# Last position tile's accumulators in three banks, and the last norm's means on VectorE

## The chip, the core and the metric

The kernel runs on one core of one Trainium2 chip. The metric is the device time of one execution in microseconds (us). TensorE (PE) multiplies into eight PSUM banks of 512 float32 columns; ScalarE (ACT), VectorE (DVE) and GpSimd (POOL) do the rest; SyncE (SP) issues every DMA.

## The reference, cut to what matters

One decoder block over 256 positions of 1024 features: two attention branches merged by gates, then a gated feed-forward part with a short causal convolution, then a last norm. The change touches only the last lines:

```python
h = rmsnorm(x, ffn_norm[l])
u = causal_dwconv(h @ w_up[l], conv_w[l], conv_b[l])
x = x + (jax.nn.silu(u[..., :D_FF]) * u[..., D_FF:]) @ w_down[l]
...
return rmsnorm(x, final_norm)      # x * rsqrt(mean(x * x) + 1e-6) * final_norm
```

## The kernel before, in words

Every float32 product on TensorE is three float32r passes: each operand is split into a rounded part (hi) and the rest (lo), and hi*hi, hi*lo and lo*hi are summed in PSUM (mm3, line 333). Weights stream through SBUF once in units of 1 MB (line 345), in three raw, three hi and three lo buffers; ScalarE copies hi, VectorE subtracts lo.

The feed-forward part has 2816 hidden features, in 11 groups g of 256. For each group two up units (line 783) compute 128 + 128 features by 256 positions: 8 K tiles, 2 halves, 3 passes, so 48 products of 256 columns each, with the weights as the stationary operand. VectorE and ScalarE then convolve and gate them and leave ph and pl. A down unit (line 821) contracts the group's two K tiles into the residual: positions lie on partitions, so the stationary operand is ph or pl, 128 positions of it, and the weights move past, 512 columns at a time. Four accumulators stay open over all 11 groups: position tile tt (0 or 1) by half n (0 or 1) of the 1024 output columns, those of tile 0 in banks of the ring sc, those of tile 1 in the two banks of the ring av. The ring sc has three banks, the ring mm three, av two. A down unit goes over K outermost; the last one goes over accumulators outermost (line 835), so that the banks close one after the other.

finish(tt), line 839, ends the kernel for a position tile: per half an add of the accumulator to x2 on VectorE and a square with a sum on ScalarE; then on GpSimd two tensor_scalar that form mean + EPS and one power to -0.5; the product of all 1024 columns with the norm's weights fn on VectorE; then y times r, 640 columns on VectorE and 384 on ScalarE, each stored by a DMA of its own from SP's queue. y is the tile B8 (B in the rows), x2 and fn lie in the tile gate, sums and means in smalls, squares go to tb.

Nothing is emitted in the order in which it is recorded. A planner (Program, lines 143 to 256) gives each instruction a price (line 277), and each engine in turn takes the oldest of its recorded instructions whose operands are there by those prices: 0.8 us after the last product for what reads TensorE's results, 0.15 us after another engine's instruction. SP alone keeps the order of recording. Instructions run in the emitted order on their engine and wait there for their operands. Everything is emitted from line 242, so all rows have that line and are told apart by tiles. These are the prices that matter, for n columns:

```python
return passes * max(0.107, 0.0025 + args[0].shape[1] / 2400)   # TensorE
return 0.1 + n * 0.833e-3 + 0.09 * more                        # ScalarE
return 0.63 if kw.get("op") == ALU.pow else 0.15 + n * 2.25e-3 # GpSimd
return 0.1 + n * 0.52e-3                                       # VectorE tensor_scalar
return (0.13 if method == "scalar_tensor_tensor" else 0.07) + n * 1.04e-3
```

Of the kernel before, what the change touches and what calls it, by code (L numbers as in the profile page):

```python
"""Hybrid MLA + MoBA block with a ConvFFN on one core.

Every float32 product on the tensor engine is three float32r passes: both operands are split
into a part rounded to float32r and the exact rest (hi*hi + hi*lo + lo*hi, summed in PSUM).
Weights stream through SBUF once, in the order of their use, and are split on the way.
Activations stay on chip, features on partitions where they are contracted next.

MoBA: SEQ equals MOBA_BLOCK, so there is one block, none lies in the past of any query, every
selected score is masked and what is left is causal attention within the block.
"""  # L10
# [17 lines left out]
D = 1024  # L28
S = 256
# [9 lines left out]
# columns of the small parameters  # L39
# [4 lines left out]
def unit_plan():  # L44
    """The weights in the order of their use: (kind, index)."""
    plan = [("lat", 0), ("lat", 1), ("lat", 2)]
    plan += [("v", n) for n in range(4)]
    plan += [("q", 0), ("gate", 0), ("k", 0), ("gate", 1), ("q", 1), ("gate", 2), ("k", 1)]
    plan += [("q", 2), ("gate", 3), ("k", 2), ("gate", 4), ("q", 3), ("gate", 5), ("k", 3)]
    plan += [("gate", 6), ("mqk", 0), ("gate", 7), ("mv", 0), ("mqk", 1), ("ob", 0), ("mqk", 2)]  # L50
    plan += [("mqk", 3), ("ob", 1)]
    plan += [("ob", 2), ("ob", 3)]
    plan += [("oa", i) for i in range(4)]
    plan += [("out", n) for n in range(4)]
    for g in range(FT // 2):
        plan += [("up", 2 * g), ("up", 2 * g + 1)]
        if g:
            plan += [("down", g - 1)]
    plan += [("down", FT // 2 - 1)]
    return plan  # L60
# [3 lines left out]
SIZE = {"mqk": 3 * 384 + 2 * 256}  # the others have UNIT columns  # L64


def pack_weights(w_in, w_uq, w_ukv, w_o_mla, w_o_moba, w_out, w_up, w_down):
    """Layout alone: each unit as [128 rows of K, column group, K tile, columns of the group]."""
# [9 lines left out]
    # rotated halves lie 64 partitions apart: [x1, x1, x2, x2]  # L78
# [40 lines left out]
def rope_tables():  # L119
    """cos and the signed sin by [row, position]; rows r and r + 64 are a rotated pair."""  # L120
# [11 lines left out]
def constants():  # L132
    """Tables that depend on shapes alone: rope, the identity, the causal mask of a block, the
    rows of the first and of the second head in a pair's rotated tile."""
    p = np.arange(128)
    mask = np.where(p[None, :] <= p[:, None], 0.0, -1e30).astype(np.float32)
    sel = np.stack([(p // 32) % 2 == 0, (p // 32) % 2 == 1], axis=1).astype(np.float32)
    return np.ascontiguousarray(
        np.concatenate([*rope_tables(), np.eye(128, dtype=np.float32), mask, sel], axis=1)
    )  # L140


class Program:
    """Instructions, recorded in the order of the computation and emitted in the order of a
    simple model of the engines: each engine takes the oldest of its instructions whose operands
    are there. What reads or writes the same part of a tile keeps its order, and so do functions
    of the scalar engine with tables of their own."""

    LATENCY = {"tensor": 0.8}  # others 0.15
    DMA_LATENCY = 1.6  # L150

    def __init__(self, nc):
        self.nc = nc
        self.ops = []  # [engine, cost, calls, dependencies]
        self.users = {}  # tile -> [(op, region, writes)]
# [8 lines left out]
    def together(self):  # L164
        """Instructions of one engine that stay together."""
# [42 lines left out]
    def emit(self):  # L208
# [16 lines left out]
        for _ in range(n):  # L225
            best = None
            for e, js in open_ops.items():
                if not js:
                    continue
                if e == "sync":  # a queue  # L230
                    js = [j for j in js if j == min(loads)]
                    if not js:
                        continue
# [36 lines left out]
def region(ap):  # L270
    """Partitions and elements of a tile that an access covers."""
# [5 lines left out]
def price(engine, method, args, kw):  # L277
    """Microseconds, about."""
# [20 lines left out]
def hybrid_block(ctx: ExitStack, tc: tile.TileContext, xT, x, par, con, fnorm, wpack, out):  # L299
# [9 lines left out]
    class Ring:  # L309
        """Tiles that take turns."""  # L310
# [32 lines left out]
    units = iter(range(len(PLAN)))  # L343

    def weights(kind, i, *cuts):
        """The next unit's two parts, split in pieces that end at the cuts."""
# [56 lines left out]
    def rsqrt(dst, src, n, width):  # L403
        """(src / n + EPS) ** -0.5"""
# [13 lines left out]
    def to_rows(o, col2):  # L418
        """[128 positions, 2] -> the same S values on every partition, in PSUM o [128, S]."""
# [5 lines left out]
    def feature_tile(o, m, w, ah, al, ks, first, last):  # L425
        """128 columns' products into half m of bank o: [features, positions]."""
# [4 lines left out]
    def proj_pair(kind, i, ah, al, *cuts):  # L431
        """Two feature tiles of 128 columns into one bank."""
# [9 lines left out]
    def proj_tokens(kind, i0, o, ah, al, *between):  # L442
        """[positions, 512 columns] in two banks, K outermost."""
# [20 lines left out]
    def rope(o, n, cos, sin):  # L464
        """o [128, n * S]; rows r and r + 64 rotate together."""
# [14 lines left out]
    # the gates' tile holds the latents before, the residual and the last weights after  # L480
# [56 lines left out]
    def lat_sums(j, tt):  # L537
        """Sums of squares over the features of a latent, by position."""
# [27 lines left out]
    # the rotated shared key, for the first and the second head of a pair: rows of the other are 0  # L566
# [11 lines left out]
    def attention(i, q, k, more, scale, vh, vl, yh, yl):  # L578
        """q, k, more: (hi, lo) of [features, 2, S]; of more queries [features, S] that the heads'
        keys, zero in the other's rows, select from."""  # L580
        heads = range(2)
        # [position of a query, its tile's keys of both heads]: 128 of the first tile, all of the second
# [28 lines left out]
        for hh in heads:  # L611
# [3 lines left out]
            # blocks (query, key): (0, 0), (1, 0), (1, 1)  # L615
# [116 lines left out]
    def to_features(ks):  # L732
        """x2's columns, features on partitions, by the norm's weights, split."""
# [24 lines left out]
    # half 0: K outermost, as the merged tiles arrive  # L758
# [5 lines left out]
    # half 1: one tile of positions after the other  # L764
# [18 lines left out]
    def up_unit(i, ph, pl):  # L783
        """u's two tiles, convolved; the gated product, split."""
# [30 lines left out]

    acc = {}
    fn = gate[:, 0:4].rearrange("p a b -> p (a b)")
    y = b8
    ss3, r3 = small(4), small(2)

    def down(g, ph, pl):
        wv = groups(weights("down", g), 2, D)
        if not acc:
            for tt in range(2):
                for n in range(2):
                    acc[tt, n] = (sc_bank, av_bank)[tt]()

        def product(tt, n, k):
            kk = 2 * g + k
            t, c = slice(128 * tt, 128 * tt + 128), slice(512 * n, 512 * n + 512)  # L830
            mm3(acc[tt, n], ph[:, k, t], pl[:, k, t], wv[0][:, 0, k, c], wv[1][:, 0, k, c],
                kk == 0, kk == FT - 1)

        order = [(tt, n, k) for k in range(2) for tt in range(2) for n in range(2)]
        for tt, n, k in order if g < FT // 2 - 1 else sorted(order):
            with P.together():
                product(tt, n, k)

    def finish(tt):
        """The last residual and norm."""  # L840
        for n in range(2):
            c = slice(512 * n, 512 * n + 512)
            dve.tensor_add(x2[:, tt, c], acc[tt, n], x2[:, tt, c])
            squares(x2[:, tt, c], ss3[:, 2 * tt + n : 2 * tt + n + 1])
        v, r = small(2), r3[:, tt : tt + 1]
        pool.tensor_scalar(v[:, 0:1], ss3[:, 2 * tt : 2 * tt + 1], 1.0 / D, EPS, op0=ALU.mult,
                           op1=ALU.add)
        pool.tensor_scalar(v[:, 1:2], ss3[:, 2 * tt + 1 : 2 * tt + 2], 1.0 / D, v[:, 0:1],
                           op0=ALU.mult, op1=ALU.add)
        pool.tensor_tensor(r, v[:, 1:2], mhalf[:, 0:1], op=ALU.pow)  # L850
        dve.tensor_mul(y[:, tt], x2[:, tt], fn)
        a, b = slice(0, 640), slice(640, D)
        dve.tensor_scalar(y[:, tt, a], y[:, tt, a], r, None, op0=ALU.mult)
        sp.dma_start(out[:, tt, a], y[:, tt, a])
        act.activation(y[:, tt, b], y[:, tt, b], AF.Copy, scale=r)
        sp.dma_start(out[:, tt, b], y[:, tt, b])
# [48 lines left out]
```

## Time and profile before

| | us |
|---|---|
| median of three runs | 450.98 |
| lowest and highest of them | 450.87, 451.32 |
| span of the profiled execution | 450.0 |
| TensorE busy in it | 439.0 (98%) |
| VectorE, ScalarE, GpSimd busy | 356.7, 274.8, 10.8 |
| TensorE's share of the chain that ended last | 96% |

The span runs from the first to the last instruction of the profiled execution; the time of a run holds a little more. TensorE's busy time is made of records whose ends are modelled and overlap. The chain that ended last goes back from the last instruction, at each step to what released it.

### The profile page before, as it was taken

The page shows a single profiled execution, that of the slowest core. Times are in us where ns is not written, and L with a number is a line of the kernel's source. Part 1 is how long each engine was busy: PE and PEld are TensorE (multiplying, and loading weights), DVE is VectorE, ACT ScalarE, POOL GpSimd, SP SyncE. Part 2 cuts the span into 40 slices and gives each one's busy share as a digit, 9 for nine tenths or more (in the row PEclk, how much of TensorE's full clock was granted, in tenths as well). Part 3 has the DMA queues.
Part 4 walks back from the last instruction along what each step waited for, and adds up shares of the span by engine and source line. Part 5 has one row for each costly group of instructions (what it writes and reads, how often), then busy time and mean ns, then how long its engine had stood idle before and what let it go on. Part 6 is the DMA issues. An engine that isn't in the chain of part 4 may idle for free.

```text
span 450.0 us, 8134 instructions
## 1 busy us (share of the span) xinstructions
PE 439.0 (98%) x3302; PEld 415.4 (92%) x3302; DVE 356.7 (79%) x548; ACT 274.8 (61%) x475; POOL 10.8 (2%) x26
## 2 busy tenths in 40 slices
PE   7999999999999999999999999999999999999993
PEld 4988999999999999999998899999999999999982
DVE  3767998888987988793788568997887797797764
ACT  5786446546554766877765558765565565565523
POOL 0010300000000000000000010000000000000002
PEclk9999999999999999999999999999999999999998
DMA  6994745455254434240288454375555555556002
GB/s 197 399 402 162 263 155 184 178 183 181 90 185 165 137 124 182 93 174 17 105 340 302 188 188 137 144 288 197 190 201 203 192 205 198 197 192 233 2 1 93
DMA packets 13861, 81.77 MB, mean 182 GB/s; under 512 B 1664, under 2 KB 2560, under 8 KB 5120
## 3 DMA queue, kind: packets, MB, share of 16 engines
q1 hardware_dynamic: 13824, 81.25, 49.9%
q8 instruction: 26, 0.43, 0.4%
q14 instruction: 11, 0.09, 0.1%
HBM read 80.20 MB, written 1.05 MB: 181 GB/s over the span
## 4 chain that ended last, share of the span: by engine, by line
PE 96%; DMA 1%; SPq 1%; ACT 1%; POOL 1%; issue 0%; DVE 0%; POOLq 0%; ACTq 0%
PE mm L242 69%; PE av L242 14%; PE sc L242 12%; DMA raw<-in_wpack 1%; SPq L242 1%; POOL smalls L242 1%; ACT tb L242 0%; DVE gate L242 0%; ACT B L242 0%; POOLq L900 0%; ACT whi L242 0%; POOLq L242 0%; ACTq L242 0%
## 5 line engine op out<-in xcount | busy, mean ns | idle before, releaser
L242 ACT CAST whi<-raw 128x1024 fp32r<-128x1024 f32 (+3 forms) x158 | 152.3, 978 | 86.0 <-PE mm L242 70.3
L242 DVE TENSOR_TENSOR wlo<-raw,whi 128x1024 fp32r<-128x1024 f32 (+3 forms) x158 | 175.8, 1129 | 34.6 <-ACT whi L242 33.9
L242 PE MATMUL mm<-XH,whi 128*128 128x256 f32 x656 | 184.4, 281 | 1.8 <-ACT whi L242 1.8
L242 PE MATMUL mm<-XH,wlo 128*128 128x256 f32 x656 | 182.7, 278 | 0.0
L242 PE MATMUL mm<-XL,whi 128*128 128x256 f32 x656 | 182.5, 278 | 0.0
L242 PEld LDWEIGHTS mm<-XH,whi 128*128 128x128 f32 x656 | 124.3, 189 | 2.7 <-ACT whi L242 2.3
L242 PEld LDWEIGHTS mm<-XL,whi 128*128 128x128 f32 x656 | 124.2, 189 | 0.5
L242 PEld LDWEIGHTS mm<-XH,wlo 128*128 128x128 f32 x656 | 124.4, 190 | 0.2 <-DVE wlo L242 0.2
L242 DVE SCALAR_TENSOR_TENSOR tb<-ta,prm,tb 128x255 f32<-128x255 f32 x88 | 40.4, 480 | 2.2 <-ACT tb L242 0.7
L242 ACT ACTIVATE tb<-ta,prm 128x256 f32<-128x256 f32 x44 | 24.3, 595 | 3.8 <-DVE ta L242 3.8
L242 ACT ACTIVATE e<-sc,smalls 128x128 f32<-128x128 f32 (+1 forms) x32 | 13.3, 419 | 12.6 <-DVE smalls L242 11.7
L242 DVE TENSOR_TENSOR ta<-ta,tb 128x256 f32<-128x256 f32 (+1 forms) x35 | 16.9, 484 | 2.2 <-ACT ta L242 0.7
L242 ACT CAST qh<-ta 128x256 fp32r<-128x256 f32 (+1 forms) x26 | 11.4, 437 | 11.8 <-DVE ta L242 11.7
L242 DVE TENSOR_TENSOR ta<-mm,rbc 128x512 f32<-128x512 f32 x22 | 15.2, 689 | 4.2 <-PE mm L242 4.2
L242 PE MATMUL mm<-YBH,whi 128*128 128x256 f32 x64 | 18.1, 283 | 0.0
L242 PE MATMUL mm<-YBH,wlo 128*128 128x256 f32 x64 | 17.7, 277 | 0.0
L242 PE MATMUL mm<-VH,whi 128*128 128x256 f32 x64 | 17.7, 277 | 0.0
L242 PE MATMUL mm<-YBL,whi 128*128 128x256 f32 x64 | 17.7, 277 | 0.0
L242 PE MATMUL mm<-VL,whi 128*128 128x256 f32 x64 | 17.7, 276 | 0.0
L242 PE MATMUL mm<-VH,wlo 128*128 128x256 f32 x64 | 17.7, 276 | 0.0
L242 PE MATMUL sc<-whi,ql 128*128 128x512 f32 x44 | 17.3, 394 | 0.0
L242 PE MATMUL av<-whi,ql 128*128 128x512 f32 x44 | 17.3, 394 | 0.0
(167 smaller groups left out, 735.1 us busy)
## 6 DMA issues: line engine op xcount, KB each, us to landing
raw<-in_wpack SPq DMA_DIRECT2D x66, 1024.0 KB, 4.8
raw<-in_wpack SPq DMA_DIRECT2D x4, 832.0 KB, 4.2
raw<-in_wpack SPq DMA_DIRECT2D x7, 256.0 KB, 6.6
raw<-in_wpack SPq DMA_DIRECT2D x2, 512.0 KB, 5.2
B<-in_x SPq DMA_DIRECT2D x1, 1024.0 KB, 10.0
gate<-in_x SPq DMA_DIRECT2D x1, 1024.0 KB, 4.8
raw<-in_xT SPq DMA_DIRECT2D x3, 256.0 KB, 6.1
cst<-in_con SPq DMA_DIRECT2D x1, 641.0 KB, 11.1
```

The source lines that it names most:

```text
L242: getattr(getattr(self.nc, e), method)(*args, **kw)
```

## The change

The accumulators become five parts: tile 0 keeps two banks of 512 columns (both sc), tile 1 gets 512 and 256 columns in the two av banks and 256 columns in the third sc bank. The products follow these parts, in the same order as before. In finish, the squares are scaled by D ** -0.5 each (a square of the input times 1/32), so that their sums are means; VectorE adds EPS to the first mean, adds the means up, and multiplies each part with the norm's weights when it is there; GpSimd keeps only the power. The final scaling is in three cuts, 0 to 384 and 384 to 640 on VectorE, 640 to 1024 on ScalarE, with the same two stores. Comments were also taken out of the file, which moves its lines.

```diff
+    parts = [(0, slice(0, 512)), (0, slice(512, D)),
+             (1, slice(0, 512)), (1, slice(512, 768)), (1, slice(768, D))]
     acc = {}
...
-    ss3, r3 = small(4), small(2)
+    r3 = small(2)
...
         if not acc:
-            for tt in range(2):
-                for n in range(2):
-                    acc[tt, n] = (sc_bank, av_bank)[tt]()
-
-        def product(tt, n, k):
+            for j, b in enumerate((sc_bank, sc_bank, av_bank, av_bank, sc_bank)):
+                acc[j] = b()
+
+        def product(j, k):
             kk = 2 * g + k
-            t, c = slice(128 * tt, 128 * tt + 128), slice(512 * n, 512 * n + 512)
-            mm3(acc[tt, n], ph[:, k, t], pl[:, k, t], wv[0][:, 0, k, c], wv[1][:, 0, k, c],
-                kk == 0, kk == FT - 1)
-
-        order = [(tt, n, k) for k in range(2) for tt in range(2) for n in range(2)]
-        for tt, n, k in order if g < FT // 2 - 1 else sorted(order):
+            tt, c = parts[j]
+            t = slice(128 * tt, 128 * tt + 128)
+            mm3(acc[j][:, : c.stop - c.start], ph[:, k, t], pl[:, k, t], wv[0][:, 0, k, c],
+                wv[1][:, 0, k, c], kk == 0, kk == FT - 1)
+
+        order = [(j, k) for k in range(2) for j in range(len(parts))]
+        for j, k in order if g < FT // 2 - 1 else sorted(order):
             with P.together():
-                product(tt, n, k)
+                product(j, k)
 
     def finish(tt):
-        """The last residual and norm."""
-        for n in range(2):
-            c = slice(512 * n, 512 * n + 512)
-            dve.tensor_add(x2[:, tt, c], acc[tt, n], x2[:, tt, c])
-            squares(x2[:, tt, c], ss3[:, 2 * tt + n : 2 * tt + n + 1])
-        v, r = small(2), r3[:, tt : tt + 1]
-        pool.tensor_scalar(v[:, 0:1], ss3[:, 2 * tt : 2 * tt + 1], 1.0 / D, EPS, op0=ALU.mult,
-                           op1=ALU.add)
-        pool.tensor_scalar(v[:, 1:2], ss3[:, 2 * tt + 1 : 2 * tt + 2], 1.0 / D, v[:, 0:1],
-                           op0=ALU.mult, op1=ALU.add)
-        pool.tensor_tensor(r, v[:, 1:2], mhalf[:, 0:1], op=ALU.pow)
-        dve.tensor_mul(y[:, tt], x2[:, tt], fn)
-        a, b = slice(0, 640), slice(640, D)
-        dve.tensor_scalar(y[:, tt, a], y[:, tt, a], r, None, op0=ALU.mult)
-        sp.dma_start(out[:, tt, a], y[:, tt, a])
-        act.activation(y[:, tt, b], y[:, tt, b], AF.Copy, scale=r)
-        sp.dma_start(out[:, tt, b], y[:, tt, b])
+
+        mine = [j for j in range(len(parts)) if parts[j][0] == tt]
+        means = small(len(mine))
+        for i, j in enumerate(mine):
+            c = parts[j][1]
+            n = c.stop - c.start
+            dve.tensor_add(x2[:, tt, c], acc[j][:, :n], x2[:, tt, c])
+            act.activation(tbs().rearrange("p a s -> p (a s)")[:, :n], x2[:, tt, c], AF.Square,
+                           scale=D ** -0.5, accum_out=means[:, i : i + 1])
+
+            if i < len(mine) - 1:
+                if i:
+                    dve.tensor_add(means[:, i : i + 1], means[:, i : i + 1], means[:, i - 1 : i])
+                else:
+                    dve.tensor_scalar(means[:, 0:1], means[:, 0:1], EPS, None, op0=ALU.add)
+                dve.tensor_mul(y[:, tt, c], x2[:, tt, c], fn[:, c])
+        v, r = small(1), r3[:, tt : tt + 1]
+        dve.tensor_add(v, means[:, -1:], means[:, -2:-1])
+        c = parts[mine[-1]][1]
+        pool.tensor_tensor(r, v, mhalf[:, 0:1], op=ALU.pow)
+        dve.tensor_mul(y[:, tt, c], x2[:, tt, c], fn[:, c])
+        cuts = (0, 384, 640, D)
+        for q, (a, b) in enumerate(zip(cuts, cuts[1:])):
+            if q < 2:
+                dve.tensor_scalar(y[:, tt, a:b], y[:, tt, a:b], r, None, op0=ALU.mult)
+            else:
+                act.activation(y[:, tt, a:b], y[:, tt, a:b], AF.Copy, scale=r)
+        sp.dma_start(out[:, tt, :640], y[:, tt, :640])
+        sp.dma_start(out[:, tt, 640:], y[:, tt, 640:])
```

## Rows read from the trace of the kernel before

**Rows 1.** The page's first line.

```profile
span 450.0 us, 8134 instructions
```

**Rows 2.** Busy time by stretch: nine feed-forward rounds; columns are named in its first line.

```profile
core 0: us, PE busy (x) PEld busy (x) DVE busy (x) ACT busy (x) POOL busy (x), PEclk, DMA share, GB/s
289.04:436.64 147.60, 147.60 (x1082) 138.74 (x1081) 121.88 (x183) 84.81 (x125) 0.00 (x0) 1.00 0.51 182
```

**Rows 3.** The chain that ended last, in order of time: start us, us, what.

```profile
420.24 10.91 PE mm L242 x96
431.15 1.37 PE sc L242 x6
...
443.49 1.16 POOL smalls L242
...
445.68 0.62 ACT B L242
```

**Rows 4.** Timeline of PE: start us, us, instruction; the last of tile 1's two accumulators.

```profile
440.37 0.39 PE L242 MATMUL av<-whi,ql 128*128 128x512 f32 x1
...
441.74 0.40 PE L242 MATMUL av<-whi,ql 128*128 128x512 f32 x1
```

**Rows 5.** Timeline of DVE in the tail.

```profile
438.06 0.69 DVE L242 TENSOR_TENSOR gate<-sc,gate 128x512 f32<-128x512 f32 x1 [2.16 <-PE sc L242]
439.43 0.69 DVE L242 TENSOR_TENSOR gate<-sc,gate 128x512 f32<-128x512 f32 x1 [0.68 <-PE sc L242]
440.15 1.23 DVE L242 TENSOR_TENSOR B<-gate 128x1024 f32<-128x1024 f32 x1
441.30 0.68 DVE L242 TENSOR_TENSOR gate<-av,gate 128x512 f32<-128x512 f32 x1
442.18 0.55 DVE L242 TENSOR_SCALAR B<-B,smalls 128x640 f32<-128x640 f32 x1 [0.20 <-POOL smalls L242]
442.65 0.69 DVE L242 TENSOR_TENSOR gate<-av,gate 128x512 f32<-128x512 f32 x1
443.37 1.23 DVE L242 TENSOR_TENSOR B<-gate 128x1024 f32<-128x1024 f32 x1
445.68 0.55 DVE L242 TENSOR_SCALAR B<-B,smalls 128x640 f32<-128x640 f32 x1 [1.09 <-POOL smalls L242]
```

**Rows 6.** Timeline of POOL in the tail.

```profile
441.60 0.55 POOL L242 TENSOR_TENSOR smalls<-smalls,mhalf 128x1 f32<-128x1 f32 x1
443.49 1.52 POOL L242 TENSOR_SCALAR smalls<-smalls 128x1 f32<-128x1 f32 x2 [1.35 <-ACT tb L242]
445.09 0.55 POOL L242 TENSOR_TENSOR smalls<-smalls,mhalf 128x1 f32<-128x1 f32 x1
```

**Rows 7.** The page's costliest groups: busy us, mean ns of one, idle before.

```profile
L242 PEld LDWEIGHTS mm<-XH,whi 128*128 128x128 f32 x656 | 124.3, 189 | 2.7 <-ACT whi L242 2.3
```

**Rows 8.** Groups by line and shape of DVE and ACT: busy us, mean ns, idle before.

```profile
L242 DVE TENSOR_TENSOR ta<-ta,tb 128x256 f32<-128x256 f32 x27 | 11.4, 423 | 2.0 <-ACT ta L242 0.7
...
L242 DVE TENSOR_SCALAR smalls<-smalls 128x2 f32<-128x2 f32 x16 | 2.7, 170 | 0.5
...
L242 DVE TENSOR_SCALAR diag<-cst,smalls 128x128 f32<-128x128 f32 x8 | 2.0, 284 | 4.1 <-POOL smalls L242 4.0
...
L242 ACT ACTIVATE ta<-tb 128x256 f32<-128x256 f32 x22 | 9.1, 413 | 2.9 <-DVE tb L242 2.8
```

**Rows 9.** Timeline of ACT: the square of tile 0's second half.

```profile
440.21 0.63 ACT L242 ACTIVATE tb<-gate 128x512 f32<-128x512 f32 x1 [0.71 <-DVE gate L242]
440.75 0.18 ACT L242 ACTIVATION_READ_ACCUMULATOR tb<-gate 128x1 f32 x1
```

**Rows 10.** Timeline: earlier powers on POOL, the DVE subtraction beside the first.

```profile
47.19 1.22 DVE L242 TENSOR_TENSOR wlo<-raw,whi 128x1024 fp32r<-128x1024 f32 x1
47.21 1.74 POOL L242 TENSOR_TENSOR smalls<-smalls,mhalf 128x2 f32<-128x2 f32 x1
...
263.52 0.69 POOL L242 TENSOR_TENSOR smalls<-smalls,mhalf 128x2 f32<-128x2 f32 x1
```

**Rows 11.** Timeline of SP's queue: the last two stores.

```profile
446.26 0.81 SPq L242 DMA_DIRECT2D out<-B  x2
```

## The prediction

> **What bounds the kernel now.** I read the page first: 450.0 us of span [rows 1]. The time to predict, 450.98 us, is the median of three runs; about 1.0 us of it lies outside the span. I make the sum on the span and keep that 1.0 us. 0.2% of the time, 0.9 us, is about what a measurement of this kernel can tell from no change. Next, the stretches: in nine rounds of the feed-forward part TensorE is busy 147.60 of 147.60 us at granted clock 1.00, its 2.4 GHz level [rows 2]. There, only what TensorE itself takes counts. Then the chain that ended last [rows 3]: TensorE all the way, then a tail that TensorE doesn't set. Its last product starts at 441.74 and is done at 442.14 [rows 4]; the last ScalarE and VectorE scalings end at 446.30 and 446.23 [rows 3, 5]. So the change can act in two places: TensorE's rounds, and the 4.1 us from its end to the last store, with some 3.7 us of store and closing behind them.
>
> The tail is seen in VectorE's rows [rows 5]. It ran add 0, add 1, weights' product of tile 0 (1.23), add 2, the scaling of tile 0 (442.18), add 3 (442.65), product of tile 1, scaling of tile 1. Add 3 could have started at 442.14 and began 0.5 late, as the scaling stood ahead of it. Behind it come two squares, two means on GpSimd and the power. Of the means the first took 1.16 us [rows 3] and the power 0.55, from 445.09 to 445.64 [rows 6].
>
> **Part 1, the shorter products.** In each of 11 down units, the 2 K tiles by 3 passes by 1 half of 512 columns make 66 products; they become 132 of 256. TensorE's price: 96 products of 256 columns took 10.91 us, 113.6 ns each; six of 512 took 1.37 us, 228.3 ns [rows 3]. Two short ones are 227.3, so 66 pairs come to 0.07 us less. The weight load of a short product lasts 189 ns [rows 7], more than 113.6, but the 96 of a round are each preceded by one and don't show it. What the trace lacks is short products whose stationary side is the activations; as bounds I take -0.1 us and, should a load show through, the third rival below. I take -0.07, as the nearest row is the same shape in the same round.
>
> The Trainium skill (TensorE: Matmul & The Clock Gate, Back-to-back issue gap) gives an isolated warm matmul N/2.4 ns plus about 2.5 ns, so each of the 66 extra products would cost that; the forecast would be 0.24 us higher, about 451.0. The trace doesn't agree: 113.6 and 228.3 ns lie 7 and 15 ns above N/2.4, an excess in proportion and not per product.
>
> The fifth accumulator takes the third of the score banks, last read at the start of the feed-forward part; nothing waits for it.
>
> **Part 2, the order.** The planner emits each engine's oldest ready instruction by its own prices (lines 208 to 256, 277 to 295), so the order can be worked out from the code. Count from its start of the last down unit: the banks close at 1.295, 2.590, 3.885, 4.540, 5.195, and an add may start 0.8 later. VectorE then takes add 0 (2.095), product 0 (2.697), add 1 (3.390), EPS, product 1 (4.093), add 2 (4.695), the sum for tile 0 (5.298), product 2 (5.369), add 3 (5.971, 256 columns). At 6.308 it is free; tile 0's power is planned out at 6.299, so tile 0's two scalings are ready and are the oldest. They go first, then tile 1's first mean, product 3, and only then add 4, ready since 5.995. The same working on the kernel before gives exactly the order of [rows 5]. ScalarE: squares 0, 1, 2, tile 0's scaling, squares 3, 4, tile 1's scaling.
>
> So add 4, whose bank closes at 442.14, still stands behind tile 0's scalings, as add 3 did, and now also behind a product. That is where I look for the gain to go.
>
> **Part 3, the tail with measured durations.** VectorE's spacing, from [rows 5]: an instruction follows an independent one 0.08 us before its end (scaling 442.18, 0.55 long; add 442.65) and one that it reads 0.03 after it. Durations: 512 columns 0.69 [rows 5], 256 columns 0.42; a scalar scaling 0.28 for 128 columns [rows 8] and 0.55 for 640 [rows 5], so by the line between them 0.42 for 384 and 0.35 for 256: the split costs two starts, 0.69 - 0.55 = 0.14 us in all. A one-column operation is not shown on VectorE; two columns take 0.17 [rows 8]; bounds 0.07 (it is overlapped) and 0.17; I take 0.17 where it is waited for, 0.07 where not. A square with its sum took 0.72 for 512 (440.21 to 440.93) [rows 9]; 256 columns save 0.63 - 0.41 [rows 8, 9], so 0.51.
>
> With TensorE's end as it was: add 1 439.43; EPS 440.04; product 1 440.15; add 2, whose bank closes at 440.76 [rows 4], 440.80; the sum for tile 0 441.41 to 441.58; product 2 441.49 to 442.18; add 3 442.10 to 442.52. GpSimd's power for tile 0 could start at 441.60, as before [rows 6], but product 2, of two SBUF operands, is running. What that does is seen earlier: a power beside a weights' subtraction (two SBUF operands, 1.22 us) took 1.74 us against 0.69 with VectorE idle [rows 10]; it ends about 0.6 after the subtraction does. The 1.16 us mean under the product at 443.37 is the same [rows 3, 5]. So the power ends 0.55 after 442.1, near 442.64, not at 442.15, and VectorE waits for it. Unknown between 0 and 0.5 us; I take it in full, as product 2 starts 0.1 earlier than the power.
>
> Scaling of 384 at 442.67, of 256 at 443.01, first mean 443.28, product 3 443.35, add 4 443.69 to 444.11 (then product 4 hidden behind the square); square 4 444.17 to 444.68; sum 444.73 to 444.90; power 444.92 to 445.47, VectorE idle beside it; scalings 445.50 and 445.84 to 446.19. Before, the last VectorE scaling ended at 446.23: -0.04. ScalarE's ends near 446.1; the two stores go out one behind the other on SP's queue as before (446.26, 0.81 for both) [rows 11], so their first one sets them.
>
> What goes: four GpSimd means, two of which were on the path (443.49 to 445.02). What takes their place: add 4, 1.55 us after its bank closed. Freed and re-spent are nearly equal. Sum: 450.98 - 0.07 - 0.04 = 450.9; I say 450.8, as the one-column operations are charged at their upper bound, 0.1 each at two places, of which I take half.
>
> **The rivals.** (a) The power isn't held up by product 2. For it: the sum for tile 0 may come out before product 2 has really begun; against it: [rows 10]. VectorE then goes from add 3 straight to the scaling at 442.44, 0.23 sooner, and all behind it: 450.6. (b) The adds follow their banks: if add 3 and add 4 are emitted ahead of tile 0's scalings, add 4 runs 442.17 to 442.59, square to 443.16, sum, power to 443.95, scalings to 444.67: 1.5 us less, 449.3. Against it: by the planner's prices the scalings are ready 0.009 us before VectorE is free, and even if they weren't, one short mean would go in between and the scalings next; only a different planned state of VectorE at the start would do it. (c) Slower: the 132 short products show their weight loads, as the loads stand at 189 ns against 113.6. At full exposure 132 x 0.075 = 9.9 us, 460.8; it decides from 7 ns for each (0.9 us), 451.9. Against it: the 96-product runs. (d) Longer queue: GpSimd gets in only after add 3 too, VectorE idle until then: 0.4 us more, 451.2.
>
> **How the numbers follow.** Forecast 0.55 (450.8, its own range 450.5 to 451.1); (a) 0.15; (b) 0.12; (c) 0.08; (d) 0.10. (a), (d) and the forecast lie within 0.2%: 0.80, less 0.01 for a low end of (a): 0.79. Faster: (b) and that 0.01, 0.13. Slower: (c), 0.08. The range reaches past (a), 450.6, by the 0.45 us between the runs shown, to 450.2, and past (d) to 451.4, leaving (b) and (c) out.
>
> **What would show it.** Right: in the chain of the changed kernel TensorE's down stretches within 0.1 us of before; on VectorE two scalings between add 3 and add 4; tile 0's power about 1.0 us long, tile 1's 0.55; tile 1's last add more than 1 us after TensorE's end; the first of the last stores issued near 446.1. Wrong: a wait of TensorE inside the rounds (its longer planned products can shift the planner's order there; one misplaced weights' subtraction is worth up to 1.2 us, hidden now since TensorE waits for nothing), a clock below 1.00, or add 4 right behind add 3.

## The result, and the profile after

The changed kernel takes 455.8 us (median of six runs, 454.95 to 457.44) against 451.15 before in the same runs: a ratio of 1.0098, 95% interval 1.0078 to 1.0119. It is slower by 1%, outside the range of the prediction. The profiled execution's span is 454.1 us against 450.0. Two executions among those of the experiments (742.71 and 743.44 us, granted clock 0.56) are in none of the ratios.

The chain that ended last shows where it goes. One round of the feed-forward part after (start us, us, what):

```profile
288.88 11.31 PE mm L242 x96
300.19 1.40 PE sc L242 x6
301.59 1.05 PE av L242 x6
302.65 1.74 PE sc L242 x9
304.39 1.03 PE av L242 x6
305.41 0.34 PE sc L242 x3
305.75 11.31 PE mm L242 x96
```

A round takes 16.87 us (288.88 to 305.75) instead of 16.40 [rows 2, 3]; nine of them make 4.2 us. Most of it is in the first line: 96 products of two up units, which the change doesn't touch, take 11.31 us instead of 10.91 [rows 3], 117.8 ns each instead of 113.6. The down part has grown too, from 5.49 (16.40 - 10.91) to 5.56 (16.87 - 11.31). Its last products, ahead of the next stretch, are at the old spacing again (the last line ahead of 305.75: three of 256 columns in 0.34 us), so each round takes up the wider spacing anew. Busy time by stretch, two rounds after and the first of these rounds before:

```profile
core 0: us, PE busy (x) PEld busy (x) DVE busy (x) ACT busy (x) POOL busy (x), PEclk, DMA share, GB/s
288.88:305.75 16.87, 16.87 (x129) 16.09 (x128) 16.62 (x25) 10.20 (x16) 0.00 (x0) 1.00 0.76 283
305.75:322.63 16.88, 16.88 (x129) 16.10 (x128) 13.53 (x21) 9.64 (x14) 0.00 (x0) 1.00 0.55 194
```

```profile
289.04:305.44 16.40, 16.40 (x123) 15.42 (x122) 16.15 (x25) 10.18 (x16) 0.00 (x0) 1.00 0.75 285
```

TensorE is busy throughout, at granted clock 1.00 as before [rows 2], and no wait of TensorE stands in the trace in these rounds: the products simply follow each other more widely. The load around them doesn't explain it: a round with 0.76 of the DMA time and one with 0.55 take the same, and before, 0.75 went with 16.40. Below, "narrow" and "wide" are the two spacings: 113.6 and 117.8 ns for 256 columns, 228.3 and 233.3 (1.40 us for six) for 512. Said of a product itself, "short" is 256 and "wide" 512 columns.

The tail, by contrast, is as forecast. TensorE's last product, VectorE and GpSimd after:

```profile
445.94 0.28 PE L242 MATMUL sc<-whi,ql 128*128 128x256 f32 x1
```

```profile
445.50 0.15 DVE L242 TENSOR_TENSOR smalls<-smalls 128x1 f32<-128x1 f32 x1
445.62 0.69 DVE L242 TENSOR_TENSOR B<-gate 128x512 f32<-128x512 f32 x1
446.23 0.42 DVE L242 TENSOR_TENSOR gate<-av,gate 128x256 f32<-128x256 f32 x1
446.75 0.68 DVE L242 TENSOR_SCALAR B<-B,smalls 128x384 f32<-128x384 f32 x2
447.35 0.15 DVE L242 TENSOR_SCALAR smalls<-smalls 128x1 f32<-128x1 f32 x1
447.42 0.42 DVE L242 TENSOR_TENSOR B<-gate 128x256 f32<-128x256 f32 x1
447.75 0.42 DVE L242 TENSOR_TENSOR gate<-sc,gate 128x256 f32<-128x256 f32 x1
...
449.63 0.68 DVE L242 TENSOR_SCALAR B<-B,smalls 128x384 f32<-128x384 f32 x2 [0.67 <-POOL smalls L242]
```

```profile
445.73 0.99 POOL L242 TENSOR_TENSOR smalls<-smalls,mhalf 128x1 f32<-128x1 f32 x1 [181.68 <-DVE smalls L242]
449.04 0.55 POOL L242 TENSOR_TENSOR smalls<-smalls,mhalf 128x1 f32<-128x1 f32 x1 [2.32 <-DVE smalls L242]
```

Tile 0's scalings (446.75) stand between add 3 (446.23) and add 4 (447.75), whose bank closed at 446.22. Tile 0's power took 0.99 us under the product at 445.62, tile 1's 0.55 with VectorE idle. From TensorE's end to the end of the last VectorE scaling: 446.22 to 450.31, 4.09 us; before, 442.14 to 446.23 [rows 4, 5], 4.09.

### The profile page after: what moved, and what is told of

The parts are those of the page before. It is cut to its first block, busy times and chain, and to the rows that moved or that the text cites. A ratio compares the mean times of both kernels' runs of the same rounds, so it can differ in the third digit from the quotient of the medians.

```text
span 454.1 us, 8273 instructions
## 1 busy us (share of the span) xinstructions
PE 443.2 (98%) x3368; PEld 422.0 (93%) x3368; DVE 358.3 (79%) x559; ACT 274.8 (61%) x477; POOL 9.3 (2%) x22
## 4 chain that ended last, share of the span: by engine, by line
PE 95%; DMA 1%; issue 1%; DVE 1%; SPq 1%; POOL 0%; POOLq 0%; ACT 0%; DVEq 0%
PE mm L242 69%; PE sc L242 13%; PE av L242 13%; DMA raw<-in_wpack 1%; SPq L242 1%; DVE B L242 0%; DVE gate L242 0%; POOL smalls L242 0%; POOLq L915 0%; ACT whi L242 0%; DVEq L915 0%; DVE smalls L242 0%
## 5 line engine op out<-in xcount | busy, mean ns | idle before, releaser
L242 PE MATMUL sc<-whi,ql 128*128 128x512 f32 (+1 forms) x66 | 23.5, 356 | 0.0
L242 PE MATMUL sc<-wlo,qh 128*128 128x512 f32 (+1 forms) x66 | 23.5, 355 | 0.0
L242 PE MATMUL sc<-whi,qh 128*128 128x512 f32 (+1 forms) x66 | 23.5, 355 | 0.0
```

The costliest lines, as they stand in the source:

```text
L242: getattr(getattr(self.nc, e), method)(*args, **kw)
```

## The experiments

In what follows a stretch is the 96 products of two up units, a seam the step from a down unit to the next up unit. Nine seams lead to a stretch. "Seam products" are what stands between two stretches.

**The tail alone** (e1_tail_only): four accumulators as before, the new finish.

```diff
-             (1, slice(0, 512)), (1, slice(512, 768)), (1, slice(768, D))]
+             (1, slice(0, 512)), (1, slice(512, D))]
...
-            for j, b in enumerate((sc_bank, sc_bank, av_bank, av_bank, sc_bank)):
+            for j, b in enumerate((sc_bank, sc_bank, av_bank, av_bank)):
```

> The new last residual and norm alone, on four accumulators of 512 columns as before. The changed kernel's feed-forward rounds take 16.87 us against 16.40 before, and every product in most of them stands 4 to 5 ns further from the next, those of the unchanged up units too. Theory A (the short products of the down units bring it on): rounds of 16.40 again, 113.6 ns per product in the stretches of 96, and the time within 0.3 us of before, 450.7 to 451.3. Rival R (the new tail's code or the planner's order brings it on): rounds near 16.87, 454 to 456.

Measured 450.89 against 451.64, ratio 0.9983 (0.9964 to 1.0002); all stretches narrow. Theory R falls. Its tail is even shorter than that of before: TensorE's end at 441.28, last scaling's end at 444.67, 3.39 us against 4.09. The last add starts 0.03 us after its bank has closed (before 0.51, in the changed kernel 1.53), and without GpSimd's means 0.38 us pass from the last square to the power (before 0.94). So the new tail alone is worth 0.70 us, and the fifth add takes that back. Timelines of PE and of DVE:

```profile
440.88 0.40 PE L242 MATMUL av<-whi,ql 128*128 128x512 f32 x1
```

```profile
441.31 0.69 DVE L242 TENSOR_TENSOR gate<-av,gate 128x512 f32<-128x512 f32 x1
441.92 0.68 DVE L242 TENSOR_SCALAR B<-B,smalls 128x384 f32<-128x384 f32 x2
...
443.99 0.68 DVE L242 TENSOR_SCALAR B<-B,smalls 128x384 f32<-128x384 f32 x2 [0.67 <-POOL smalls L242]
```

**As many short products at two places** (e2_split_k0, e3_split_k1): the kernel before, one product of tile 1's second half cut in two, for the first K tile or the second (K stands for 0 or 1 in the edit).

```diff
-            mm3(acc[tt, n], ph[:, k, t], pl[:, k, t], wv[0][:, 0, k, c], wv[1][:, 0, k, c],
-                kk == 0, kk == FT - 1)
+            cuts = (0, 256, 512) if (tt, n, k) == (1, 1, K) else (0, 512)
+            for p, q in zip(cuts, cuts[1:]):
+                d = slice(512 * n + p, 512 * n + q)
+                mm3(acc[tt, n][:, p:q], ph[:, k, t], pl[:, k, t], wv[0][:, 0, k, d],
+                    wv[1][:, 0, k, d], kk == 0 and p == 0, kk == FT - 1)
```

> The kernel before; only the product of tile 1's second half is cut into two of 256 columns, in the same bank, and only for the first K tile of each group, so products of 512 columns follow it and stand ahead of the up unit's stretch. 33 products more. Theory A1 (the wide spacing sets in where a product of 256 columns stands right before the up unit's first product, and then holds): rounds of 16.40, time 450.8 to 451.4. Rival A2 (it is the number of products or weight loads): half of the changed kernel's loss, 453. Rival A3 (the fifth open bank): 451, since there is none.

> As the one with the first K tile cut, but cut for the second K tile instead, so the round's down products end with six of 256 columns right ahead of the up unit. As many products. A1: stretches of 96 at 117.8 ns, rounds near 16.85, time 454 to 456. A2: 453, like its twin. A3 (the fifth bank): 451.

K = 0: 451.69 against 451.64, ratio 1.0010 (0.9994 to 1.0026), all stretches narrow. K = 1: 453.81, ratio 1.0052 (1.0033 to 1.0071). Its stretches alternate, by the chain:

```profile
371.93 10.89 PE mm L242 x96
382.82 1.37 PE sc L242 x6
384.19 1.37 PE av L242 x6
385.57 1.37 PE sc L242 x6
386.94 1.37 PE av L242 x9
388.31 11.31 PE mm L242 x96
399.62 1.40 PE sc L242 x6
```

The twins issue the same products, and nothing but the place of six short ones differs. The time of the second alone would also have suited A2 (453); its twin and the chain decide. So the count (A2) is out, and a loss comes without a fifth bank (A3). A1 had the sign and place right, but not that every other stretch stays narrow.

**The wide part last** (e4_wide_last): the changed kernel, another order in the rounds.

```diff
-        order = [(j, k) for k in range(2) for j in range(len(parts))]
+        order = [(j, k) for k in range(2) for j in (0, 1, 3, 4, 2)]
```

> The changed kernel; in the rounds (not in the last down unit) tile 1's 512-column part is multiplied last in each K tile, behind its two of 256. As many products, five banks. A1: stretches back at 113.6 ns, rounds of 16.40, time 450.7 to 451.4. A2 and A3: as the changed kernel, 455 to 456.

Measured 451.65 against 451.64, ratio 1.0004 (0.9986 to 1.0022). The whole loss is gone with the same products and five banks, which leaves neither A2 nor A3:

```profile
368.19 1.37 PE sc L242 x6
369.56 0.34 PE av L242 x3
369.90 0.34 PE sc L242 x3
370.24 0.69 PE av L242 x3
370.93 10.91 PE mm L242 x96
```

The six short products take 0.68 us, the three wide ones 0.69, and a round 16.39 against 16.40: the short ones cost nothing here, as the prediction had it.

**Added products at the seam** (e7_one_wide, e8_one_short, f1_two_wide, f2_three_wide, f3_two_short, f4_wide_before): behind each down unit but the last, one to three products are added to the changed kernel or to the one before, of 512 or 256 columns, with the passes' operands in turn; the results are thrown away. The edit for one of 512:

```diff
+        if g < FT // 2 - 1:
+            free = mm_bank.tiles[mm_bank.n % 3]
+            mm(free, ph[:, 1, 128:256], wv[0][:, 0, 1, 0:512], True, True)
```

> The changed kernel with one product of 512 columns more at each seam from a down unit to the next up unit, ten in all, whose result is thrown away (the next unit's bank is written anew). The six of 256 still stand ahead of it. Theory A1 (the direct predecessor of the unit's first product decides): stretches of 96 at 113.6 ns; ten times 0.229 us are added and the 4.2 us lost in the rounds come back, so near 454. Rival A4 (a run of short products at the end of the round decides, whatever comes between): 117.8 ns, near 458.

> The kernel before with one product of 256 columns more at each of the ten seams, its result thrown away. Ten times 0.114 us is 1.1 us. A1: that one product is enough for the wide spacing; if the seam switches from either state to the other, as it did with the second K tile cut (every other stretch at 117.8), five rounds of 0.45 us come on top, 455; if it always ends wide, ten rounds, 457. A4: 452.8, since one short product is no run.

> The changed kernel with two products of 512 columns more (first and second pass, results thrown away) at each of the ten seams from a down unit to an up unit: 20 times 0.229 us, 4.6 us. With one, every other stretch was wide; theory A1 as put (the direct predecessor decides) has fallen. Theory W (a run of products of 512 columns ahead of the seam brings the narrow spacing back; one is too short, the three of the wide-last kernel were enough): with two either all stretches at 113.6 ns, 456.3, or still some at 117.8. Theory P (the parity of the number of products between two stretches decides: even keeps the state, odd switches it; 32 here): the same spacing in all stretches, as in the changed kernel 117.8, 460.4.

> The same with three, all passes: 6.9 us more. Theory W: as in the wide-last kernel all stretches at 113.6 ns, 458.5. Theory P (33, odd): every other stretch at 117.8, 460.7.

> The kernel before with two products of 256 columns more at each seam: 2.3 us. With one, every other stretch was wide. Theory W with a switch (each seam with short products ahead of it turns the spacing over): every other stretch again, 456.2. Theory P (26, even): all stretches alike, 453.9 or 458.4.

> The kernel before with one product of 512 columns more at each seam: 2.3 us. Theory W: 25 wide ones ahead of the seam, all stretches at 113.6 ns, 453.9. Theory P (25, odd): every other stretch at 117.8, 456.2. Theory L (any added product that writes the next unit's bank does it): wide stretches here too.

| kernel | us, against before | ratio (interval) | stretches behind seams |
|---|---|---|---|
| changed, one wide more | 456.09, 451.68 | 1.0108 (1.0085 to 1.0131) | every other wide |
| changed, two wide more | 456.78, 451.83 | 1.0102 (1.0072 to 1.0131) | all narrow |
| changed, three wide more | 458.42, 451.83 | 1.0152 (1.0114 to 1.0189) | all narrow |
| before, one short more | 454.86, 451.68 | 1.0074 (1.0057 to 1.0090) | every other wide |
| before, two short more | 458.95, 451.83 | 1.0158 (1.0121 to 1.0195) | all wide |
| before, one wide more | 455.81, 451.83 | 1.0097 (1.0063 to 1.0131) | every other wide |

One wide more on the changed kernel fits neither A1 (454) nor A4 (458), and one short more on the one before not A4 (452.8). The times agree with the states. Two short ones, for instance: 20 x 0.113 for the products themselves, and nine rounds whose stretch is 0.40 and whose 24 down products are 4 x 0.03 longer, 2.3 + 4.7 = 7.0; measured 7.1. The chains of two short and of one wide more, both on the kernel before:

```profile
359.39 11.54 PE mm L242 x98
370.93 1.40 PE sc L242 x6
372.33 1.40 PE av L242 x6
```

```profile
372.16 11.13 PE mm L242 x97
383.30 1.37 PE sc L242 x6
384.67 1.37 PE av L242 x6
386.04 1.37 PE sc L242 x6
387.42 1.37 PE av L242 x6
388.79 11.54 PE mm L242 x97
```

(98 = 2 short and 96; 97 = 1 wide and 96: 11.13 - 0.23 = 10.90 and 11.54 - 0.23 = 11.31.) The last one is the strongest: all seam products are wide, and still every other stretch is wide. So A1, the width of the direct predecessor, has fallen, and so has W, a run of wide ones; parity (P), which fits two short and one wide more, falls by three more on the changed kernel, 33 and all narrow.

**Count or operands** (g1_third_pass, g2_two_wide_before, g3_three_wide_before): the kernel before with one wide product of the third pass, with two, and with three more; one execution each. The edit of the first:

```diff
+            mm(free, pl[:, 1, 128:256], wv[0][:, 0, 1, 0:512], True, True)
```

> The kernel before with one product of 512 columns more at each seam, this time of the third pass (stationary ql, moving hi), where the earlier one was of the first pass (qh, hi) and made every other stretch wide. Theory C (the number of products ahead of the seam counts, whatever their operands): every other stretch at 117.8 ns again, 456. Theory O (which operands the last product had): as its round now ends with the same pass as before, all stretches at 113.6, 454.

> The kernel before with two more of 512 columns at each seam, first and second pass: 4.6 us. Theory C by parity (26, even) or as on the changed kernel with two: all stretches at 113.6, 456.3. If wide stretches appear, the count that matters isn't the parity.

> The kernel before with three more of 512 columns, all passes: 6.9 us. By sets of three (a whole set ends the round): all stretches at 113.6, 458.5. By parity (27, odd): every other at 117.8, 460.7.

One of the third pass: 456.43 against 450.76, every other stretch wide, as with one of the first pass: the number counts, not the operands of the last product. Two: 455.61, all narrow, so theory L (any added product does it) is out. Three: all narrow, which rules out parity on this base too; its one time, 461.29, isn't used, as that execution came to its first such stretch 2.7 us later (291.71) than the profiled one of before (289.04).

Over all kernels whose seam ends with wide products, their number since the last short one tells the state: a whole multiple of three (24 before, in the tail alone and in the four-bank version below; 12 with K = 0 cut; 3 with the wide part last and with three added to the changed kernel; 27) or two more (2, 26) is narrow throughout; one more (1, 25, 25) makes every other stretch wide. Ending with short ones, one behind 24 wide and six behind 21 alternate; two behind 24 and six behind nine (the changed kernel) are always wide. That is a regularity of these kernels.

The traces hold something of the same length. Their starts, read to the nanosecond, give products of 512 columns at the narrow spacing a cycle: about 226, 229 and 232 ns from start to start, over and over. Where such products stand ahead of a seam and end on a whole cycle, or on its second step, the stretch is narrow; where they end on the first step (226 or 227 ns), it is wide. (One wide more on the changed kernel, with short ones just ahead of it, fits only in part.) With one wide product more on the kernel before, the down unit behind a wide stretch begins its cycle only with its sixth product, so that the next seam falls on a second step: such a kernel alternates. No run was made to test this, and what in TensorE keeps the cycle or the state stays open.

**Versions that keep the gain of the tail** (e5_adds_first_five, e6_adds_first_four): the tail recorded in steps over both tiles, so that tile 1's adds are older than tile 0's scalings for the planner: sums (adds and squares), power (means and power), weigh (the norm's weights), scale (times r). The edit, without the four functions' bodies:

```diff
...
-    for tt in range(2):
-        finish(tt)
+    for step in (sums, power, weigh, scale):
+        for tt in range(2):
+            step(tt)
```

> Five accumulators, the wide part of tile 1 last in the rounds, and the tail recorded in another order: adds and squares of both tiles, then means and powers, then the products with the norm's weights, then the scalings (640 columns in one on VectorE). The planner then puts add 3 and add 4 ahead of tile 0's scaling. By the working of the second rival (b): the last scaling ends 2.6 us after TensorE instead of 4.1, so 1.5 us less than before, 450.1 against 451.6. If the tail is bound by something else (the store, ScalarE), within 0.5 us of before.

> The same recording order with four accumulators of 512 columns. The last add takes 0.69 instead of 0.42 us and the last square 0.72 instead of 0.51, so the last scaling ends about 3.0 us after TensorE: 0.4 us more than with five, 1.1 us less than before, 450.5.

Five accumulators, wide part last: 450.91 against 451.68, ratio 0.9985 (0.9969 to 1.0002). Four: 450.83, ratio 0.9984 (0.9970 to 0.9999), faster than before by the narrowest margin. The gains fell short of the expected 1.5 and 1.1 us. Five, timelines of PE and DVE:

```profile
442.49 0.28 PE L242 MATMUL sc<-whi,ql 128*128 128x256 f32 x1
```

```profile
442.12 0.42 DVE L242 TENSOR_TENSOR gate<-av,gate 128x256 f32<-128x256 f32 x1
442.46 0.68 DVE L242 TENSOR_TENSOR B<-gate 128x512 f32<-128x512 f32 x1
443.06 0.42 DVE L242 TENSOR_TENSOR gate<-sc,gate 128x256 f32<-128x256 f32 x1
...
444.39 0.55 DVE L242 TENSOR_SCALAR B<-B,smalls 128x640 f32<-128x640 f32 x1
444.85 0.15 DVE L242 TENSOR_TENSOR smalls<-smalls 128x1 f32<-128x1 f32 x1
445.67 0.55 DVE L242 TENSOR_SCALAR B<-B,smalls 128x640 f32<-128x640 f32 x1 [0.67 <-POOL smalls L242]
```

Add 4 is no longer behind the scalings, but behind a 0.68 us product (442.46), and tile 1's last sum (444.85) now stands behind tile 0's scaling (444.39). TensorE ended at 442.77, the last scaling at 446.22: 3.45 us, 0.6 less than before. With four:

```profile
441.59 0.40 PE L242 MATMUL av<-whi,ql 128*128 128x512 f32 x1
```

```profile
444.64 0.55 DVE L242 TENSOR_SCALAR B<-B,smalls 128x640 f32<-128x640 f32 x1 [0.67 <-POOL smalls L242]
```

From 441.99 to 445.19, 3.20 us. The tail alone had 3.39 without any new order of recording, so the order, with the scaling in one piece, is worth 0.2 us with four accumulators, and the three times (450.89, 450.91, 450.83) can't be told apart.

## Why the prediction was wrong

- **Part 1, the price of the short products: this step failed.** I took -0.07 us for the 66 pairs, from one spacing for 256 columns and one for 512. The products I priced cost what I said (the wide-last kernel shows it: 0.68 against 0.69 us). But I took the spacing of every other product in the rounds as given. Where the short products stand, it isn't: 96 unchanged products a round went from 113.6 to 117.8 ns, and the term came out at +4.2 us (nine times 0.40 in the stretch and 0.07 in the down unit). My sum lacked a term, the spacing of what follows.
- The row that contradicts a single spacing was in the trace of before, in the chain of an earlier stage, and I hadn't looked for it:

```profile
107.44 2.83 PE mm L242 x24
```

  2.83 / 24 is 117.9 ns, for the same shape as the 113.6 of [rows 3], at granted clock 1.00 too. A size with two prices in one trace is a size whose price depends on something else.
- **Rival (c)** was the one on the right side, and for the wrong reason. It put the loss on 132 products whose weight loads show. By that, the wide-last kernel with the same 132 would have lost as much, and the twin cut at K = 0 as much as its sibling; neither lost anything that shows. The wide spacing adds about as much to a product of 512 columns (228.3 to 233.3) as to one of 256 (113.6 to 117.8), and a load of 189 ns [rows 7] is no limit at 228.
- The Trainium skill's rule that I weighed (TensorE: Matmul & The Clock Gate, Back-to-back issue gap), about 2.5 ns for each isolated product beside its columns, would have given 0.17 us for 66 more products. No run agrees with that as the cost of this change: the wide-last kernel shows none (16.39 us a round against 16.40), the changed one 4.2 us.
- **Part 2, the order** was right throughout: two scalings between add 3 and add 4, and the power's place. **Part 3, the tail** too: power 0.99 (forecast 1.04), the second 0.55, last add 1.53 behind its bank (forecast 1.55); the tail's change was forecast at -0.04 us and measured as 0.00 (4.09 and 4.09). That was no luck: each step came within 0.05 us of its place behind TensorE's end. The half of 0.1 us that I had still taken off for the one-column operations wasn't there: they took 0.15, near the upper bound of 0.17.
- **Rivals (a) and (d)** are out by the power's 0.99 us. **(b)** was not this kernel. When recorded so that the adds come early, five accumulators gave 0.6 us of shorter tail and not the 1.5 of its working, which had left out what the planner then puts ahead of the last add and the last sum.
- What I named as a sign of error, a wait of TensorE inside the rounds or a clock below 1.00, didn't come; the rounds grew with neither. What I named as signs of being right came true beside a wrong forecast, "down stretches within 0.1 us" (5.56 against 5.49) among them: they looked at the products that change and not at their neighbours. The range was too narrow because the chance of 0.08 for slower came from one mechanism alone.

## What to carry to other kernels

Where one engine is busy without a gap, a change of its instruction stream is priced by the spacing of all that follows, not only of what is changed: read the spacing of the same shape in several stretches first, and if it differs, count every product of the stage as exposed. After any cut of products, compare the length of a stretch that the change doesn't touch; 11.31 against 10.91 us is seen at once in the chain. And where a new order in the round is free, try one: putting the wide product last gave all 4.2 us back.

## What the runs showed of the hardware

Matmuls of 256 columns follow each other at 113.6 or 117.8 ns, of 512 at 228.3 or 233.3, at the same granted clock 1.00; a stretch of 96, its first few products aside, stays in one of the two, and the products between two stretches, by their number and widths, set which, in the one trace kept of each of these kernels. At the narrow spacing products of 512 go in a cycle of about 226, 229 and 232 ns. A power of one column on GpSimd takes 0.55 us with VectorE idle and 0.99 us when VectorE began a product of two SBUF operands 0.11 us earlier (445.62 and 445.73); a product that began 0.18 us after the power left it at 0.55 (442.28 and 442.46, adds first with five accumulators).
